# Both parts of the input in one product of 512 columns, joined at eviction

## The chip, the cores and the metric

The kernel runs on one core of a Trainium2 chip. The metric is the device time of one execution in microseconds (us), lower is better. The core's engines that matter here are TensorE (PE in the profile, with its weight loads shown apart as PEld), VectorE (DVE), ScalarE (ACT) and the DMA queue that SyncE (SP) issues to. Products are accumulated in PSUM, which has eight banks; a bank holds 512 fp32 values a partition. All other tiles are in SBUF.

## What is computed

Two layers of a hybrid network over 256 tokens (128 of context, 128 latent), `D_MODEL` = 2048, `DEPTH` = 2. Nearly all the arithmetic of a layer is a matrix product of an activation with a weight that is read from HBM once:

```python
h = rms_norm(x, p['g_mix']) * (1 + scale1) + shift1
z = h @ p['w_in']                                   # 2048 -> 10752
q, k, v, xr, xg, us, gl = jnp.split(z, offs, axis=-1)
...                                                 # attention, RG-LRU scan, S5 scan
ssm = ssm * jax.nn.sigmoid(ssm @ p['glu_w'] + p['glu_b'])
merged = (g[:, :, 0] * (attn @ p['w_pa']) + g[:, :, 1] * (rec @ p['w_pr'])
          + g[:, :, 2] * (ssm @ p['w_ps']))
x = x + gate1 * (merged @ p['w_o'])
a, b = jnp.split(h2 @ p['w_up'], 2, axis=-1)        # h2: second norm
x = x + gate2 * ((jax.nn.gelu(dwconv_centred(a, ...)) * b) @ p['w_down'])
```

Scale, shift and gate come from a modulation product with `w_mod` (2048 -> 12288 a layer). All is fp32.

## The kernel before

**Split products.** To get fp32 accuracy out of the one-pass format `float32r`, each operand is kept as two parts: a rounded one (hi) and the rest (lo). For each contraction tile of 128 the kernel makes three products into one PSUM tile of 128 outputs x 256 tokens: weight-hi x input-hi, weight-hi x input-lo, weight-lo x input-hi. In all three the weight part (128 x 128) is the stationary operand and the input part (128 x 256) streams. `mm3` writes this for a unit of 16 contraction tiles (48 products, one bank); `unit2` for two output tiles of 8 contraction tiles each (24 products in each of two banks):

```python
a, b = xh(kt), xl(kt)
self.mm(pt, hi[:, c], a, kt == 0, False)
self.mm(pt, hi[:, c], b, False, False)
self.mm(pt, lo[:, c], a, False, kt == KT - 1)
```

The input's hi and lo parts lie in different tiles: `H0`/`H1` (hi) and `H2`/`H3` (lo) for the normed input, `brh`/`brl` for a branch's result, `hh`/`hl` for the hidden layer, `xas` for the input that is used before its norm is known (`early`).

**The stream of weights.** `run_items` walks a list of items. A "w" item is a unit; a "mod" item is one piece of the modulation product (into PSUM tile `ps_md`, four products of 32 rows side by side in plain fp32, which the trace records as eight); `filler` puts about 0.9 of them after each unit. Each half of a unit's weights (512 KB) is loaded by SP into one of six `raw` buffers (`emit_dma`), split by ACT (`whi`, a CAST, L115) and DVE (`wlo`, a subtraction, L71) in `emit_split`; three pairs of split buffers exist, so the split of a half waits until PE has read the half three before.

**Evictions.** The result of a unit is taken out of PSUM one item later (`later(1, ...)`), by a function that belongs to the unit: a tanh or a copy on ACT, a multiply-add on DVE, several instructions in some. Tag `mm` has two banks, so a bank has to be free two banks later. Evictions read PSUM (`ps_mm`) directly.

**Side work.** Between units `feed` advances generators that issue the S5 scan (`s5_gen`, in layer 0 also its tables, `s5_prep`), the attention and the RG-LRU scan, mostly DVE and some ACT work, at fixed steps a unit. The order on each engine is then made by a scheduler.

The stages by time in the trace: start-up to 160 us; layer 0's input projection, branches and S5 to 760; the rest of layer 0's mixing part and its channel part (`w_up`, `w_down`) to 1640; layer 1's mixing part to 2330; its rest to 3124.

Of the kernel before, what the change touches and what calls it, by code (L numbers as in the profile page):

```python
# [5 lines left out]
F32 = mybir.dt.float32  # L6
F32R = mybir.dt.float32r
# [4 lines left out]
P = 128  # L12
L = 2
D = 2048
KT = 16
# [18 lines left out]
class Builder:  # L34
# [150 lines left out]
    def emit_split(self, i, h):  # L185
        """parts of half a unit for the fp32r products; False while the buffers are still to be read"""
# [110 lines left out]
    # standard K=2048 unit, one 128-wide output tile  # L297
    def unit(self, src, xh, xl, evac):
# [6 lines left out]
    def mm3(self, pt, hv, xh, xl):  # L305
        for kt in range(KT):
            hi, lo = hv[kt // 8]
            c = slice((kt % 8) * P, (kt % 8 + 1) * P)
            a, b = xh(kt), xl(kt)
# [5 lines left out]
    def unit2(self, src, xh, xl, evac):  # L315
        def mm(hv):
            for t in range(2):
                pt = self.ps("mm", [T], 2)
                for kt in range(8):
                    hi, lo = hv[t]  # L320
                    c = slice(kt * P, (kt + 1) * P)
                    a, b = xh(kt), xl(kt)
                    self.mm(pt, hi[:, c], a, kt == 0, False)
                    self.mm(pt, hi[:, c], b, False, False)
                    self.mm(pt, lo[:, c], a, False, kt == 7)
                self.later(1, lambda t=t, pt=pt: evac(t, pt))
# [6 lines left out]
    def mod_mm(self, pt, raw, g, a, start, stop):  # L333
        """four contraction tiles at once, each in its own rows; only the first rows of a group are of use"""
# [17 lines left out]
    def mod_chunk(self, v, q, then):  # L352
        """two output tiles of a vector of layer 0, for use at once"""
# [22 lines left out]
    def startup(self, begin, evs, begin2, evs2):  # L376
        """the first norm, the S5 input and the first heads of layer 0, as the chunks of its scale and shift come in"""
# [21 lines left out]
        for q in range(8):  # L399
# [11 lines left out]
            def mm(hv, q=q):  # L411
                xh, xl = self.hx()
                for j in range(2):
                    hi, lo = hv[j]
                    kt = 2 * q + j
                    for f in range(8):
                        c = slice(f * P, (f + 1) * P)
                        self.mm(acc[f], hi[:, c], xh(kt), kt == 0 and f % 2 == 0, False, skip_group_check=True)
                        self.mm(acc[f], hi[:, c], xl(kt), False, False, skip_group_check=True)
                        self.mm(acc[f], lo[:, c], xh(kt), False, kt == KT - 1, skip_group_check=True)  # L420
# [9 lines left out]
            def mm2(hv, q=q):  # L430
                xh, xl = self.hx()
                for j in range(4):
                    hi, lo = hv[j // 2]
                    kt = 2 * q - 2 + j
                    for f in range(4):
                        c = slice((4 * (j % 2) + f) * P, (4 * (j % 2) + f + 1) * P)
                        self.mm(acc[8 + f], hi[:, c], xh(kt), kt == 0 and f % 2 == 0, False, skip_group_check=True)
                        self.mm(acc[8 + f], hi[:, c], xl(kt), False, False, skip_group_check=True)
                        self.mm(acc[8 + f], lo[:, c], xh(kt), False, kt == KT - 1, skip_group_check=True)
# [66 lines left out]
    def h_begin(self):  # L506
        self.H = [self.st(f"H{j}", [8, T], F32R, name=f"h{j}") for j in range(4)]
# [27 lines left out]
    def norm_part(self, l, which, kts, rs=None):  # L535
# [4 lines left out]
        for kt in kts:  # L540
            t = self.XA[kt // 8][:, kt % 8, :]
            hi, lo = self.H[kt // 8][:, kt % 8, :], self.H[2 + kt // 8][:, kt % 8, :]
# [1036 lines left out]
```

## Time and profile before

| | |
|---|---|
| time, median of 3 runs | 3125.14 us (3122.89 to 3130.1) |
| span of the profiled execution | 3124.1 us |
| PE busy / PEld busy | 98% / 91% of the span |
| DVE busy / ACT busy | 68% / 50% |
| mean granted TensorE clock | 0.997 of 2.4 GHz |
| HBM traffic | 231 GB/s over the span |

The span runs from the first to the last instruction of the profiled execution; what lies around it is about 1 us of the median. A busy share counts overlapping instructions once. Matmuls overlap one another, so PE's busy share says that a product was always under way, not that the engine was at its peak: the rate is read from the distance between the starts of successive products. Windows are given in us from the start of the span.

### The profile page before, as it was taken

The numbers are of one execution on the slowest core, as the hardware profiler recorded it, in microseconds if no ns is written. First come the engines' busy times: TensorE is split into PE (matmuls) and PEld (weight loads), VectorE is DVE, ScalarE is ACT, GpSimd is POOL, SyncE is SP. The second block draws the span as 40 slices with busy tenths as digits, with TensorE's granted clock in tenths as the row PEclk, the third lists the DMA queues.
The fourth block names the chain that finished last, engine by engine and source line by source line (L and its number), as shares of the span: only waits on it lengthen the run. The fifth ranks groups of instructions, "written<-read, shape, count | busy, mean of one in ns | idle before, by whom it ended". The sixth has DMA issues, their size and how long they took to land.

```text
span 3124.1 us, 66739 instructions
## 1 busy us (share of the span) xinstructions
PE 3063.2 (98%) x27745; PEld 2831.5 (91%) x27745; DVE 2125.4 (68%) x3864; ACT 1558.4 (50%) x2434; POOL 45.9 (1%) x87
## 2 busy tenths in 40 slices
PE   5899999999999999999999999999999999999999
PEld 4788888998999999999998888888999999999999
DVE  6478899989465766667557677877644766555554
ACT  4455767345445643344456446674334565434443
POOL 0000000000000000000000000000000000000000
PEclk9999999999999999999999999999999999999999
DMA  9865666667777777777777777777775546555553
GB/s 351 322 205 191 209 210 216 214 223 247 254 236 234 269 264 257 257 264 250 271 258 246 244 248 235 255 252 267 266 256 197 184 164 212 179 188 177 185 186 129
DMA packets 188542, 724.48 MB, mean 232 GB/s; under 512 B 21520, under 2 KB 22064, under 8 KB 179280
## 3 DMA queue, kind: packets, MB, share of 16 engines
q1 hardware_dynamic: 180576, 691.95, 65.0%
q0 software_dynamic: 7664, 28.27, 2.4%
q8 instruction: 218, 3.57, 0.4%
q14 instruction: 84, 0.69, 0.1%
HBM read 704.46 MB, written 15.68 MB: 231 GB/s over the span
## 4 chain that ended last, share of the span: by engine, by line
PE 87%; DVE 3%; ACT 2%; DMA 2%; issue 1%; SPq 0%; DVEq 0%; ACTq 0%
PE ps_mm L118 77%; PE ps_md L118 5%; PE ps_aux L118 2%; DMA raw<-in_w_in 2%; PE ps_y L118 1%; PE ps_v L118 1%; DVE wlo L71 1%; ACT whi L115 1%; PE ps_v L121 0%; ACT ltmp L111 0%; DVE t L71 0%; ACT xa L111 0%; PE ps_aux L121 0%; DVE xs L925 0%; DVE blk L71 0%
## 5 line engine op out<-in xcount | busy, mean ns | idle before, releaser
L118 PE MATMUL ps_mm<-h,whi 128*128 128x256 f32 x9824 | 1807.3, 286 | 5.8 <-ACT whi L115 4.1
L118 PEld LDWEIGHTS ps_mm<-h,whi 128*128 128x128 f32 x9824 | 1531.0, 192 | 90.7 <-issue 59.6
L115 ACT CAST whi<-raw 128x1024 fp32r<-128x1024 f32 x896 | 936.8, 1046 | 1303.1 <-PE ps_mm L118 1100.1
L71 DVE TENSOR_TENSOR wlo<-raw,whi 128x1024 fp32r<-128x1024 f32 x896 | 1095.3, 1223 | 684.8 <-ACT whi L115 662.6
L118 PE MATMUL ps_mm<-h,wlo 128*128 128x256 f32 x4912 | 1392.5, 284 | 9.3 <-DVE wlo L71 9.3
L118 PEld LDWEIGHTS ps_mm<-h,wlo 128*128 128x128 f32 x4912 | 942.4, 192 | 14.7 <-DVE wlo L71 11.7
L118 PE MATMUL ps_mm<-hh,whi 128*128 128x256 f32 x1024 | 292.8, 286 | 0.0
L118 PE MATMUL ps_mm<-hl,whi 128*128 128x256 f32 x1024 | 289.7, 283 | 0.0
L118 PE MATMUL ps_mm<-hh,wlo 128*128 128x256 f32 x1024 | 289.6, 283 | 0.0
L118 PE MATMUL ps_mm<-brh,whi 128*128 128x256 f32 x896 | 257.8, 288 | 0.0
L118 PE MATMUL ps_mm<-brl,whi 128*128 128x256 f32 x896 | 254.3, 284 | 0.0
L118 PE MATMUL ps_mm<-brh,wlo 128*128 128x256 f32 x896 | 253.1, 283 | 0.0
L118 PEld LDWEIGHTS ps_mm<-hh,whi 128*128 128x128 f32 x1024 | 196.2, 192 | 11.9 <-issue 11.1
L118 PE MATMUL ps_md<-raw,SC 128*32 128x256 f32 x2560 | 201.5, 389 | 2.1 <-issue 1.9
L118 PEld LDWEIGHTS ps_mm<-hl,whi 128*128 128x128 f32 x1024 | 196.4, 192 | 0.0
L118 PEld LDWEIGHTS ps_mm<-hh,wlo 128*128 128x128 f32 x1024 | 196.4, 192 | 0.0
L118 PEld LDWEIGHTS ps_mm<-brh,whi 128*128 128x128 f32 x896 | 171.4, 191 | 17.4 <-issue 10.7
L118 PEld LDWEIGHTS ps_mm<-brl,whi 128*128 128x128 f32 x896 | 171.6, 192 | 0.9 <-issue 0.8
L118 PEld LDWEIGHTS ps_mm<-brh,wlo 128*128 128x128 f32 x896 | 171.5, 192 | 0.1
L84 DVE SCALAR_TENSOR_TENSOR x<-ps_mm,MOD,x 128x128 f32<-128x128 f32 x192 | 58.6, 347 | 69.0 <-PE ps_mm L118 69.0
L118 PEld LDWEIGHTS ps_md<-raw,SC 128*32 128x32 f32 x2560 | 58.3, 108 | 46.2 <-issue 14.0
L111 ACT ACT_TABLE_LOAD x73 | 93.7, 1283 | 11.2 <-DVE sm L84 4.1
(238 smaller groups left out, 2631.6 us busy)
## 6 DMA issues: line engine op xcount, KB each, us to landing
raw<-in_w_mod SPq DMA_DIRECT2D x384, 512.0 KB, 5.1
raw<-in_w_in SPq DMA_DIRECT2D x304, 512.0 KB, 5.1
raw<-in_w_up SPq DMA_DIRECT2D x166, 512.0 KB, 4.5
raw<-in_w_up SPq DMA_DIRECT2D x45, 1024.0 KB, 4.9
raw<-in_w_down SPq DMA_DIRECT2D x90, 512.0 KB, 4.6
raw<-in_w_o SPq DMA_DIRECT2D x64, 512.0 KB, 4.6
raw<-in_w_down SPq DMA_DIRECT2D x19, 1024.0 KB, 4.9
raw<-in_w_pa SPq DMA_DIRECT2D x32, 512.0 KB, 5.1
```

What stands on the lines that cost most here:

```text
L71: self.nc.vector.tensor_tensor(out=out, in0=a, in1=b, op=op)
L84: self.nc.vector.scalar_tensor_tensor(out=out, in0=a, scalar=s, in1=b, op0=op0, op1=op1)
L111: self.nc.scalar.activation(out, a, func, **k)
L115: self.nc.scalar.copy(out, a)
L118: self.nc.tensor.matmul(out, lhsT, rhs, start=start, stop=stop, **k)
```

## The change

`unit`, `unit2` and `early` no longer issue two products with the weight's hi part. The input's two parts lie side by side (`split`: tiles of 4 contraction tiles x 2 parts x 256), and one product of 512 columns makes both, into the two halves of a bank that is now used whole. The product with the weight's lo part is added onto the first half (`mmx`); in the last contraction tile it goes first. At eviction `joined` copies the second half to SBUF by ACT and adds the first half to it by DVE; the unit's own eviction then reads that SBUF tile (`pj`) in place of PSUM. The start-up's products (`mmy`) and those of the V projection stay three of 256 columns.

```diff
     def unit(self, src, x, evac):
         def mm(hv):
-            pt = self.ps("mm", [T], 2)
-            self.mm3(pt, hv, xh, xl)
-            self.later(1, lambda: evac(pt))
+            pt = self.ps("mm", [2, T], 2)
+            self.mm3(pt, hv, x)
+            self.later(1, lambda: evac(self.joined(pt)))
...
-            self.mm(pt, hi[:, c], a, kt == 0, False)
-            self.mm(pt, hi[:, c], b, False, False)
-            self.mm(pt, lo[:, c], a, False, kt == KT - 1)
+            self.mmx(pt, hi[:, c], lo[:, c], x(kt), kt == 0, kt == KT - 1)
+    def mmx(self, pt, hi, lo, x, first, last):
+        if last:
+            self.mm(pt[:, 0, :], lo, x[:, 0, :], False, False)
+        self.mm(pt, hi, x, first, last)
+        if not last:
+            self.mm(pt[:, 0, :], lo, x[:, 0, :], False, False)
...
+    def joined(self, pt):
+        t = self.k1("pj")
+        self.acp(t, pt[:, 1, :])
+        self.add(t, pt[:, 0, :], t)
+        return t
+
+    def split(self, tags, name):
+        ts = [self.st(t, [4, 2, T], F32R, name=name) for t in tags]
+        return lambda kt: ts[kt // 4][:, kt % 4]
...
     def unit2(self, src, x, evac):
-                pt = self.ps("mm", [T], 2)
+                pt = self.ps("mm", [2, T], 2)
...
-                self.later(1, lambda t=t, pt=pt: evac(t, pt))
+                self.later(1, lambda t=t, pt=pt: evac(t, self.joined(pt)))
...
     def h_begin(self):
-        self.H = [self.st(f"H{j}", [8, T], F32R, name=f"h{j}") for j in range(4)]
+        self.H = self.split([f"H{j}" for j in range(4)], "h")
...
             def out():
                 t = box["t"] = self.k1("ee")
-                self.acp(t, pt)
+                self.acp(t, pt[:, 1, :])
+                self.add(t, pt[:, 0, :], t)
```

Over the whole program there are 6,912 products of 512 columns in place of twice as many of 256, and 482 joins (one ACT copy and one DVE addition each).

PE in the last part of layer 1, where one unit of `w_down` ends and the next begins (`ps_mm` is the bank, `hh`/`hl` are hidden-hi and hidden-lo, the column at the end is the product's size). Before:

```order
L118 MATMUL ps_mm_37130<-hh1_34204,whi_37119 128x256
L118 MATMUL ps_mm_37130<-hl1_34206,whi_37119 128x256
L118 MATMUL ps_mm_37130<-hh1_34204,wlo_37120 128x256
L118 MATMUL ps_mm_37186<-hh0_34203,whi_37123 128x256
L118 MATMUL ps_mm_37186<-hl0_34205,whi_37123 128x256
L118 MATMUL ps_mm_37186<-hh0_34203,wlo_37124 128x256
```

The same place in the changed kernel (`hid` holds both parts):

```order
L118 MATMUL ps_mm_31690<-hid_29364,wlo_31677 128x256
L118 MATMUL ps_mm_31690<-hid_29364,whi_31676 128x512
L118 MATMUL ps_mm_31690<-hid_29364,wlo_31677 128x256 x2
L118 MATMUL ps_mm_31690<-hid_29364,whi_31676 128x512
L118 MATMUL ps_mm_31733<-hid_29361,whi_31680 128x512
L118 MATMUL ps_mm_31733<-hid_29361,wlo_31681 128x256
```

Three products and three loads of weights a contraction tile became two and two, and the unit ends with a product of 512.

DVE in layer 0's first branch, at the eviction of the seventh `unit2` of `w_pa` (`mg` is the merged sum, `tg` the gate, `H`, `t`, `blk`, `FIN` belong to the S5 scan and its tables). Before:

```order
L71 TENSOR_TENSOR H<-pc,pd 128x2x130 x2
L84 SCALAR_TENSOR_TENSOR mg_3292<-tg,ps_mm 128x256
L71 TENSOR_TENSOR wlo<-raw,whi 128x1024
L95 COPY FIN<-H 128x4
L71 TENSOR_TENSOR t_5415<-blk,TINY 128x512
L71 TENSOR_TENSOR t_5416<-blk,TINY 128x512
L84 SCALAR_TENSOR_TENSOR mg_3292<-tg,ps_mm 128x256
L71 TENSOR_TENSOR blk<-t_5415,t_5416 128x256 x2
```

In the changed kernel:

```order
L71 TENSOR_TENSOR wlo<-raw,whi 128x1024
L95 COPY FIN<-H 128x4
L71 TENSOR_TENSOR t_4975<-blk,TINY 128x512
L71 TENSOR_TENSOR t_4976<-blk,TINY 128x512
L71 TENSOR_TENSOR pj<-ps_mm,pj 128x256
L71 TENSOR_TENSOR blk<-t_4975,t_4976 128x256 x2
L84 SCALAR_TENSOR_TENSOR mg_3110<-tg,pj 128x256
L71 TENSOR_TENSOR pj<-ps_mm,pj 128x256
L71 TENSOR_TENSOR wlo<-raw,whi 128x1024
L84 SCALAR_TENSOR_TENSOR mg_3110<-tg,pj 128x256
```

Each of the two evictions has got an addition of its own ahead of the multiply-add, and the bank is released by that addition.

## Rows read from the trace of the kernel before

**Rows 1.** Page, part 1: busy time of each engine, share, instructions.

```profile
PE 3063.2 (98%) x27745; PEld 2831.5 (91%) x27745; DVE 2125.4 (68%) x3864; ACT 1558.4 (50%) x2434; POOL 45.9 (1%) x87
```

**Rows 2.** Chain that ended last, 2330 to 3124 us: start, duration, engine, count.

```profile
2330.32 230.39 PE ps_mm L118 x1920
```

**Rows 3.** Busy time by stage; after the engines clock, DMA share, GB/s.

```profile
0.00:160.00 160.00, 120.31 (x1108) 94.65 (x1109) 83.49 (x257) 68.39 (x145) 4.30 (x11) 0.95 0.89 336
160.00:330.00 170.00, 167.51 (x1515) 147.87 (x1513) 137.30 (x285) 93.56 (x167) 3.40 (x6) 1.00 0.58 191
330.00:760.00 430.00, 426.33 (x4191) 385.30 (x4189) 397.03 (x853) 252.47 (x377) 11.29 (x21) 1.00 0.66 221
760.00:1640.00 880.00, 880.00 (x7848) 811.92 (x7847) 554.34 (x988) 399.76 (x618) 16.80 (x31) 1.00 0.75 256
1640.00:2330.00 690.00, 680.11 (x6460) 604.60 (x6460) 492.79 (x848) 371.99 (x597) 8.45 (x15) 1.00 0.75 253
2330.00:3124.00 794.00, 788.94 (x6636) 787.16 (x6634) 460.49 (x636) 372.25 (x534) 1.61 (x3) 1.00 0.54 180
```

**Rows 4.** The same stretches, instructions on tile ps_mm alone: PE, PEld, DVE, ACT.

```profile
160.00:330.00 170.00, 125.39 (x960) 117.67 (x960) 12.22 (x26) 10.17 (x24) 1.00 0.58 191
330.00:760.00 430.00, 344.74 (x2743) 332.38 (x2744) 12.33 (x30) 16.29 (x43) 1.00 0.66 221
760.00:1640.00 880.00, 805.85 (x6439) 779.40 (x6438) 77.00 (x201) 25.91 (x52) 1.00 0.75 256
1640.00:2330.00 690.00, 541.84 (x4262) 518.87 (x4261) 25.32 (x58) 31.53 (x81) 1.00 0.75 253
2330.00:3124.00 794.00, 785.91 (x6529) 784.08 (x6528) 77.88 (x203) 26.61 (x54) 1.00 0.54 180
```

**Rows 5.** Timeline of PEld near 284 us, loads for plain fp32 products of 512 columns.

```profile
283.65 0.19 PEld L118 LDWEIGHTS ps_aux<-attf,kv 128*128 128x128 f32 x1 [0.24 <-issue]
284.08 0.19 PEld L118 LDWEIGHTS ps_aux<-attf,kv 128*128 128x128 f32 x1 [0.24 <-issue]
```

**Rows 6.** Timeline of PE: four plain fp32 products of 256, then twelve of 1.

```profile
412.63 1.02 PE L118 MATMUL ps_aux<-xc,gw 128*128 128x256 f32 x4
...
171.56 1.48 PE L118 MATMUL ps_aux<-CST,sqq 128*128 128x1 f32 x12
```

**Rows 7.** Groups of PE by form: last, mean ns of one product.

```profile
L118 PE MATMUL ps_mm<-hl,whi 128*128 128x256 f32 x1024 | 289.7, 283 | 0.0
L118 PE MATMUL ps_aux<-xc,gw 128*128 128x256 f32 x128 | 32.9, 384 | 2.5 <-ACT ltmp L111 2.5
L121 PE MATMUL ps_v<-CST,S 128*128 128x128 f32 x128 | 19.4, 273 | 2.0 <-ACT vs L115 1.5 <-DVE pb L71 0.5
L118 PE MATMUL ps_aux<-CST,sqq 128*128 128x1 f32 x64 | 8.7, 247 | 2.5 <-ACT sqq L111 2.3
```

**Rows 8.** Groups by form of ACT and DVE that stand for the join.

```profile
L115 ACT COPY kv<-ps_mm 128x256 f32<-128x256 f32 x8 | 2.7, 368 | 0.0
L71 DVE TENSOR_TENSOR fa<-fa,ps_mm 128x256 f32<-128x256 f32 x62 | 26.1, 420 | 35.2 <-PE ps_mm L118 35.2
L71 DVE TENSOR_TENSOR hl<-fa,hh 128x256 fp32r<-128x256 f32 x64 | 26.7, 419 | 1.0 <-ACT hh L115 1.0
```

**Rows 9.** Busy time in the two stretches where DVE is fullest.

```profile
510.00:560.00 50.00, 49.66 (x461) 44.94 (x454) 49.62 (x105) 30.73 (x48) 0.55 (x1) 1.00 0.66 223
710.00:760.00 50.00, 49.18 (x488) 43.69 (x487) 49.01 (x129) 26.97 (x43) 1.61 (x3) 1.00 0.73 248
```

**Rows 10.** Chain that ended last, 1640 to 1800 us, around one wait.

```profile
1729.87 0.61 PE ps_md L118 x8
1730.49 0.02 issue
1730.50 6.55 DMA raw<-in_w_in
```

**Rows 11.** Timeline of ACT and DVE, 2700 to 2709 us: splits and evictions in w_up.

```profile
2700.10 1.05 ACT L115 CAST whi<-raw 128x1024 fp32r<-128x1024 f32 x1 [1.88 <-PE ps_mm L118]
2701.17 1.23 DVE L71 TENSOR_TENSOR wlo<-raw,whi 128x1024 fp32r<-128x1024 f32 x1 [1.70 <-ACT whi L115]
2702.93 1.05 ACT L115 CAST whi<-raw 128x1024 fp32r<-128x1024 f32 x1 [1.32 <-PE ps_mm L118]
```

More of the change, by code (lines that the diff above doesn't have):

```diff
@@ L295, in run_items, with unit, mm3 @@
         self.run_pending(10 ** 9)
-    def unit(self, src, xh, xl, evac):
+    def unit(self, src, x, evac):
         def mm(hv):
-            pt = self.ps("mm", [T], 2)
-            self.mm3(pt, hv, xh, xl)
-            self.later(1, lambda: evac(pt))
+            pt = self.ps("mm", [2, T], 2)
+            self.mm3(pt, hv, x)
+            self.later(1, lambda: evac(self.joined(pt)))
         self.items.append(dict(ffn=self.ffn, kind="w", src=src, mm=mm))
-    def mm3(self, pt, hv, xh, xl):
+    def mm3(self, pt, hv, x):
         for kt in range(KT):
@@ L308, in mm3, with mmy, unit2 @@
             c = slice((kt % 8) * P, (kt % 8 + 1) * P)
-            a, b = xh(kt), xl(kt)
-            self.mm(pt, hi[:, c], a, kt == 0, False)
-            self.mm(pt, hi[:, c], b, False, False)
-            self.mm(pt, lo[:, c], a, False, kt == KT - 1)
-    def unit2(self, src, xh, xl, evac):
+            self.mmx(pt, hi[:, c], lo[:, c], x(kt), kt == 0, kt == KT - 1)
[5 more added lines that the diff above has]
+            self.mm(pt[:, 0, :], lo, x[:, 0, :], False, False)
+    def mmy(self, pt, hi, lo, x, first, last, **k):
+        self.mm(pt, hi, x[:, 0, :], first, False, **k)
+        self.mm(pt, hi, x[:, 1, :], False, False, **k)
+        self.mm(pt, lo, x[:, 0, :], False, last, **k)
+    def joined(self, pt):
[6 more added lines that the diff above has]
+        return lambda kt: ts[kt // 4][:, kt % 4]
+    def unit2(self, src, x, evac):
         def mm(hv):
             for t in range(2):
-                pt = self.ps("mm", [T], 2)
+                pt = self.ps("mm", [2, T], 2)
                 for kt in range(8):
@@ L417, in mm @@
                         c = slice(f * P, (f + 1) * P)
[L418 to L420 removed]
+                        self.mmy(acc[f], hi[:, c], lo[:, c], x(kt), kt == 0 and f % 2 == 0, kt == KT - 1, skip_group_check=True)
                 def out():
@@ L565, in xa_begin @@
             return
-        xs = [self.st(t, [8, T], F32R, name="xas") for t in split]
-        self.XSPL = (lambda kt: xs[kt // 8][:, kt % 8, :]), (lambda kt: xs[2 + kt // 8][:, kt % 8, :])
+        self.XSPL = self.split(split, "xas")
     def xa(self, kt):
@@ L574, in xa @@
         if self.XSPL:
[L575 removed]
+            h = self.XSPL(kt)
+            self.hilo(h[:, 0], h[:, 1], t)
     def early(self, l, which, src, evac):
@@ L611, in early, with br_begin, bx @@
         return scale, lambda: evac(box["t"])
+    def br_begin(self):
+        self.BR = [self.st(t, [4, 2, T], F32R, name="br") for t in ("B0", "B1")]
+    def bx(self, kt):
+        return self.BR[kt // 4][:, kt % 4]
     def hx(self):
-        return (lambda kt: self.H[kt // 8][:, kt % 8, :]), (lambda kt: self.H[2 + kt // 8][:, kt % 8, :])
+        return lambda kt: self.H(kt)
     def setup(self):
@@ L1314, in ev @@
                 self.xa(o)
-            self.unit(d["w_o"][l, o], hx[0], hx[1], ev)
+            self.unit(d["w_o"][l, o], hx, ev)
             self.filler(1)
@@ L1327, in hid_begin @@
             def hid_begin():
-                self.HID = [self.st("A0", [8, T], F32R, name="hh0"), self.st("A1", [8, T], F32R, name="hh1"),
-                            self.st("B0", [8, T], F32R, name="hl0"), self.st("B1", [8, T], F32R, name="hl1")]
+                self.HID = self.split(("A0", "A1", "B0", "B1"), "hid")
             evs = []
@@ L1360, in layer @@
                     self.seg = 3
-                self.unit(evs[k][0], hx[0], hx[1], evs[k][1])
+                self.unit(evs[k][0], hx, evs[k][1])
                 self.filler(1)
@@ L1382, in ev @@
                             q.dma_start(dst[:, o + 1 - w:o + 1, :], self.X[o // 8][:, (o + 1 - w) % 8:(o + 1 - w) % 8 + w, :])
-                self.unit(d["w_down"][l, hf, o], dx[0], dx[1], ev)
+                self.unit(d["w_down"][l, hf, o], lambda kt: self.HID(kt), ev)
                 self.filler(1)
@@ L1405, in win_unit @@
     def win_unit(self, l, c, hx, ev):
-        self.unit(self.d["w_in"][l, c], hx[0], hx[1], ev)
+        self.unit(self.d["w_in"][l, c], hx, ev)
         self.filler(1)
```

67 lines of the change are left out of this document (30 added, 37 removed).

## The prediction

> **What bounds the kernel now.** I read the page's busy shares first, then the chain of waits, then a table by stage. PE is busy 98% of the span, DVE 68%, ACT 50% [rows 1]. In the last part of layer 1 the chain is PE alone, 1,920 products in 230.39 us, so 0.120 us from one start to the next [rows 2]. The stages differ [rows 3]. From 760 to 1640 and from 2330 to 3124 PE is the bound: DVE holds 554 of 880 us and 460 of 794. From 330 to 760 PE and DVE are both full: DVE holds 397 of 430 us, and 49.6 and 49.0 of 50 in its fullest stretches [rows 9]. From 1640 to 2330 DVE holds 493 of 690 us, and the chain goes now and then through a weight load that lands late, 6.55 us after its issue [rows 10]. The start-up keeps its products, so nothing is taken from it.
>
> The split products make up most of PE's work. By the rows on their PSUM tile [rows 4] there are 960 from 160 to 330, 2,743 from 330 to 760, 6,439 from 760 to 1640, 4,262 from 1640 to 2330 and 6,529 after. With the V projection's 96 a layer taken out and divided by three, these are 288, 914, 2,146, 1,389 and 2,176 contraction tiles, 6,913 together; the changed program has 6,912 products of 512. Each contraction tile costs 3 x 0.120 = 0.360 us now.
>
> **What a product of 512 columns costs.** No such product of this format is in the trace. Three neighbours bound it. Plain fp32 products of 512 columns start 0.43 us apart (284.08 less 283.65), and their weight loads leave PEld idle 0.24 us each [rows 5]; four of 256 columns take 1.02 us with about 0.38 for the last, so 0.213 apart [rows 6, 7]. So plain fp32 time is proportional to columns, 0.83 ns each, with 2 or 3 ns left over. Twelve products of one column take 1.48 us with 0.247 for the last [rows 6, 7], 0.112 apart: that is what a load of 128 x 128 takes when nothing else is to be done. One split product at half the plain time per column would be 0.107 us, and measures 0.120. The 13 ns above can be
>
> - the load (0.112) that hardly fits beside 0.107 us of columns. Then 512 columns hide it, and the pair of products costs half of 0.43 and 0.120, so 0.335 us: 25 ns saved a contraction tile;
> - a fixed cost a product. Then the pair costs 0.227 and 0.120, so 0.347: 13 ns saved;
> - a slower rate per column in this format. Then 512 columns cost 0.240, and nothing is saved but perhaps the 3 ns that plain products leave over.
>
> The durations of single products speak for something of the product's own: 283 ns for a split product against 273 for a plain one of 128 columns, whose columns also take 0.107 us [rows 7], so some 10 ns, with the load the same size. That is against the first reading in part, and leaves the second and third. The first two agree that 512 columns are better than twice 256, by 13 to 25 ns; I take 18, nearer to the row on durations, so 0.342 us a pair.
>
> **The rest of the change.** Each of the 482 results costs ACT a copy of half a bank, 0.368 us, and DVE an addition of 0.420 [rows 8]: 177 us of ACT and 202 of DVE over the kernel. What the unit's own eviction reads from SBUF in place of PSUM I cost at nothing, since a subtraction on SBUF tiles of 256 columns runs 0.419 us, as long as the product with PSUM beside it [rows 8].
>
> - **760 to 1640 and 2330 to 3124** (PE-bound, 4,322 contraction tiles): 4,322 x 18 ns = 78 us less. The join lies beside PE's work: a half's weights are split by a CAST of 1.05 us and a subtraction of 1.23 us, which end 2.3 us after the third half before is read [rows 11], and they are needed two halves (5.76 us) after it. The copy and the addition stand ahead of them in ACT's and DVE's queue and take at most 0.9 us of those 3.4. A bank is needed again one unit later, and is free a little over 1 us after the last product. If that cover were gone, each join would cost PE its 0.8 us, 386 us over the 482.
> - **160 to 330**: 288 x 18 ns = 5 us; DVE rises from 137 to about 145 of 170, I take 4 less.
> - **330 to 760**: PE could save 914 x 18 ns = 16 us. But DVE gets 73 joins (30 evictions on DVE and 43 on ACT read the tile there, one instruction each [rows 4]) x 0.420 = 31 us, and its 397 us become 428 in a stretch of 430. Queued behind each addition are the weight's lo part and the S5 scan, and PE waits for the lo part. In its fullest stretches DVE reached 0.98 to 0.99 of the time, over the whole stage 0.92. At 0.99 the stage lasts 432 us, at 0.92 it lasts 465; I take 0.96, so 446: 16 us more.
> - **1640 to 2330**: 1,389 x 18 ns = 25 us, DVE has room. Where the chain goes through a late load, a faster PE only waits longer, so I keep half: 12 us less. The order in which SP issues loads stays as it is, and each load is freed by the same split.
> - **Ends**: the last result needs the copy and the addition ahead of the two multiply-adds, 0.8 us, and at the three places where a norm waits for the last result of a sum the same is paid once: 4 us together.
>
> The sum is 3124 - 78 - 4 + 16 - 12 + 4 = 3050 us of span; the median of the runs lies 1 us above the profiled span, so 3051.
>
> **Rivals.**
>
> 1. *The load is the whole excess* (0.335 a pair). Then the parts are 108, 6 and 17 us less, the stage from 330 to 760 costs 14 more (DVE bound either way), the ends 4: 3011 us of span, 3012. For it: a lone load takes 0.112 us, and in each plain product of 512 it is hidden by far. Against: the 10 ns in the durations. The Trainium skill, "TensorE: Matmul & The Clock Gate", section "Back-to-back issue gap", gives N/2.4 + 2.5 ns for an isolated product on a warm clock, 216 ns at 512 columns. By the page a pair would be 0.336 and the sum the same as here; the plain rows agree with its 2.5 ns (0.43 for twice 512 columns' time), the split product of 256 does not (0.120 against 109 ns by the page).
> 2. *DVE binds wherever the scan runs.* The stage from 330 to 760 goes on at DVE's 0.92, so 35 us more, and layer 1's mixing part gains nothing: 3124 - 78 - 2 + 35 + 4 = 3083, 3084 us. For it: DVE's queue is in order and an addition now waits for ACT's copy, so waits are added with the work. Against: the scheduler sets the additions between other work.
> 3. *The format's rate per column is the limit* (a pair stays at 0.357 to 0.360). Then PE-bound stages give 0 to 13 us, and the joins cost DVE's full stage 17 to 20 us, layer 1's mixing part up to 5, and 4 at the ends: 3132 to 3153 us, about 3142, so slower than before. It decides from a pair of about 0.355 us: 4,322 x 5 ns no longer pays the 22 us. For it: the trace has one size of split product only, and 0.120 / 256 would do as a rate. Against: nothing else suggests so odd a rate, 1.12 times half of the plain one.
> 4. *The wide product is not one product on the chip.* The trace has each plain fp32 product twice as often as the program: 128 on the RG-LRU gates [rows 7], where the program issues 64. If a wide split product ran as two of 256 with a load each, nothing would be saved and the joins paid: 3153 us. Against: split products of 256 stand in the trace once each, the 6,913 contraction tiles of [rows 4] show it.
>
> **Chances.** The forecast 0.38 (3035 to 3080), the load 0.22, DVE 0.12, the rate 0.25, two products 0.03. The likeliest gives 3051 us. The range goes from 3005, below the load's 3012, to 3150, which takes in most of the rate's cases; some 0.12 is left out. A measurement of this kernel can tell about 0.2% (6 us) from no change. Faster by more than that: the first three and little of the rate, 0.73. Within it: the better end of the rate, 0.08. Slower: 0.19.
>
> **What would show it.** In the changed profile the chain from 2330 on should be PE again, with starts 0.215 to 0.230 us apart after a product of 512 and about 0.120 after one of 256: that pair decides between the readings, and 0.24 would make the prediction wrong. PE's loads should be a third fewer on the split products. DVE's busy time should be about 2,330 us and ACT's 1,735. The stage that ends at 760 should end at 765 to 800; if it ends before 755, DVE was not full. From 330 to 760 waits of PE for the weights' lo part should appear; in the PE-bound stages there should be none.

## The result and the profile after

The changed kernel takes 3088.51 us (median of four runs, 3087.64 to 3091.02), the kernel before, timed beside it, 3124.01 us (3119.44 to 3130.1). The ratio is 0.9881, with a 95% interval of 0.9865 to 0.9896: 1.2% faster. The forecast was 3051 us, the range 3005 to 3150. So the sign and the range held, and about half of the forecast gain came: the profiled span went from 3124.1 to 3085.9 us, 38 us less where the sum had 74.

The busy shares, page part 1 of after (for [rows 1]):

```profile
span 3085.9 us, 53872 instructions
PE 3022.0 (98%) x20833; PEld 2443.8 (79%) x20833; DVE 2280.2 (74%) x4352; ACT 1700.4 (55%) x2910; POOL 45.8 (1%) x87
```

6,912 products and as many weight loads are gone (27,745 to 20,833), and PE is still busy 98% of the span: it had 25% fewer instructions and lost 1.3% of its busy time. DVE rose by 155 us and ACT by 142 us.

Busy time by stage in after, the stretches cut where the work of [rows 3] ends (columns: stretch, length, PE, PEld, DVE, ACT, POOL, granted clock, DMA share, GB/s):

```profile
0.00:157.00 157.00, 117.80 (x1105) 92.59 (x1106) 83.55 (x257) 68.08 (x144) 4.30 (x11) 0.96 0.89 342
157.00:327.00 170.00, 167.86 (x1240) 133.65 (x1239) 143.82 (x310) 99.09 (x185) 3.39 (x6) 0.99 0.58 194
327.00:757.00 430.00, 423.44 (x3271) 333.95 (x3270) 411.50 (x911) 274.30 (x450) 11.29 (x21) 1.00 0.65 220
757.00:1623.00 866.00, 863.04 (x5677) 687.79 (x5677) 601.76 (x1139) 441.50 (x755) 16.79 (x31) 1.00 0.75 259
1623.00:2297.00 674.00, 669.49 (x5079) 524.56 (x5078) 527.07 (x952) 404.12 (x699) 8.46 (x15) 1.00 0.76 259
2297.00:3086.00 789.00, 780.40 (x4470) 671.26 (x4468) 512.54 (x786) 413.30 (x681) 1.61 (x3) 1.00 0.53 182
```

The lengths of before were 160, 170, 430, 880, 690 and 794 us. The first surprise is the third row: the stage that was to be held up by DVE is as long as before, with DVE at 411.5 of 430. The second is the last row: 2,176 contraction tiles with PE as the bound gave 5 us by these cuts (8 by the marks of the table below), where 39 were forecast.

The chain of waits from 2700 to 3000 us in after is one piece (start, duration, engine, count):

```profile
2699.99 300.09 PE ps_mm L118 x1699
```

So PE alone, as in [rows 2], but 300.09 / 1,699 is 0.1766 us a product, 0.3533 us a pair of a wide and a narrow one. Before it was 0.360. The timeline of PE shows how the pair divides (start, duration):

```profile
2900.57 0.40 PE L118 MATMUL ps_mm<-h,whi 128*128 128x512 f32 x1
2900.81 0.28 PE L118 MATMUL ps_mm<-h,wlo 128*128 128x256 f32 x1
2900.93 0.40 PE L118 MATMUL ps_mm<-h,whi 128*128 128x512 f32 x1
2901.17 0.28 PE L118 MATMUL ps_mm<-h,wlo 128*128 128x256 f32 x1
2901.29 0.40 PE L118 MATMUL ps_mm<-h,whi 128*128 128x512 f32 x1
```

0.24 us from the start of a wide product to the next, 0.12 after a narrow one. Over all pairs on this tile the starts mostly lie 230 to 241 ns apart after a wide product (median 236) and 113 to 120 after a narrow one (median 117). A pair saves 360 - 353.3 = 6.7 ns, not 18; over 6,912 of them that is 46 us. So the products gave 46 us and, net, something took 8 back. Part of it shows in the waits of PE and PEld (waiting tile and line, released by; us in total, times, longest):

```profile
PE ps_mm L118 <- DVE pj L71: 5.9, 10, 1.2
PEld ps_mm L118 <- ACT pj L115: 36.4, 87, 1.0
PEld ps_mm L118 <- DVE pj L71: 21.6, 45, 1.7
```

`pj` is the tile of the join, and nothing like it stood in before. PEld's waits may be covered by the product that runs meanwhile, those of PE are not. By windows, PE's 5.9 us are 2.4 from 330 to 760 us, 0.9 from 1640 to 2300, 1.6 from 2300 to 2442 and one wait of 1.0 at the norm that follows; from 760 to 1640 there is none. But for the last, these are stretches with units of 1024 rows (`unit2`: `w_glu` and the three branch projections `w_pa`, `w_pr` and `w_ps`), where a bank takes 8 contraction tiles only. From 760 to 1640 such units stand too (layer 0's `w_glu` and `w_ps`), but with pieces of the modulation product between them, which give a bank more time. In layer 1's `w_glu` and `w_ps`, from 2300 to 2442, there are no such pieces; the same part of before had no wait of PE at all. Three timelines around 2412 us, in `w_ps` of layer 1, show one (start, duration, instruction, idle time before it). ACT:

```profile
2412.67 1.05 ACT L115 CAST whi<-raw 128x1024 fp32r<-128x1024 f32 x1 [1.50 <-issue]
2413.62 0.36 ACT L115 COPY pj<-ps_mm 128x256 f32<-128x256 f32 x1
```

DVE at the same place:

```profile
2413.75 1.22 DVE L71 TENSOR_TENSOR wlo<-raw,whi 128x1024 fp32r<-128x1024 f32 x1 [0.31 <-ACT whi L115]
2414.89 0.42 DVE L84 SCALAR_TENSOR_TENSOR h<-mg,h 128x256 fp32r<-128x256 f32 x1
2415.23 0.42 DVE L71 TENSOR_TENSOR pj<-ps_mm,pj 128x256 f32<-128x256 f32 x1
```

PE, the rows at the change from bank to bank:

```profile
2412.20 0.88 PE L118 MATMUL ps_mm<-br,whi 128*128 128x512 f32 x2
2415.26 1.00 PE L118 MATMUL ps_mm<-br,whi 128*128 128x512 f32 x2
```

The two rows of PE are the last wide product of one bank and the first of the next; two of them in a row take 0.63 us where nothing is waited for (0.236 from start to start and 0.40 for the second), so 0.25 and 0.37 us are wait. Such waits are mostly too short for the list above, since the product before them still counts as running: at the 37 changes of bank from 2300 to 2450 us that have two wide products in a row, the starts lie 4.9 us further apart, added up, than at 0.236 each; in e2, e4 and e7 below the same sum is nothing. A bank's last product starts at 2412.20. ACT's copy starts at 2413.62, behind the CAST of the next weights in ACT's queue, DVE's addition at 2415.23, behind that weight's low part, and the bank is free at 2415.65, 3.2 us after the last product has had its 0.24. It is needed 8 pairs after that, 2.8 us. In the units of 2048 rows the same join has 16 pairs, 5.65 us.

### The profile page after: what moved, and what is told of

It is laid out like the page before. It is cut to its first block, busy times and chain, and to the rows that moved or that the text cites. A ratio compares the mean times of both kernels' runs of the same rounds, so it can differ in the third digit from the quotient of the medians.

```text
span 3085.9 us, 53872 instructions
## 1 busy us (share of the span) xinstructions
PE 3022.0 (98%) x20833; PEld 2443.8 (79%) x20833; DVE 2280.2 (74%) x4352; ACT 1700.4 (55%) x2910; POOL 45.8 (1%) x87
## 5 line engine op out<-in xcount | busy, mean ns | idle before, releaser
L118 PE MATMUL ps_mm<-h,whi 128*128 128x512 f32 (+1 forms) x4976 | 1772.3, 400 | 10.0 <-DVE pj L71 4.7
L118 PEld LDWEIGHTS ps_mm<-h,whi 128*128 128x128 f32 x4976 | 925.9, 189 | 286.5 <-issue 29.1
L115 ACT COPY pj<-ps_mm 128x256 f32<-128x256 f32 x479 | 175.6, 367 | 377.5 <-PE ps_mm L118 377.3
L118 PE MATMUL ps_mm<-hid,whi 128*128 128x512 f32 x1024 | 364.5, 401 | 0.0
L118 PE MATMUL ps_mm<-br,whi 128*128 128x512 f32 x896 | 324.8, 405 | 2.1 <-DVE pj L71 1.2
L71 DVE TENSOR_TENSOR pj<-ps_mm,pj 128x256 f32<-128x256 f32 x479 | 200.8, 420 | 124.7 <-ACT pj L115 124.2
L118 PE MATMUL ps_mm<-hid,wlo 128*128 128x256 f32 x1024 | 277.0, 281 | 0.0
L118 PE MATMUL ps_mm<-br,wlo 128*128 128x256 f32 x896 | 233.9, 282 | 0.0
L118 PEld LDWEIGHTS ps_mm<-hid,whi 128*128 128x128 f32 x1024 | 190.3, 188 | 53.5 <-ACT pj L115 7.8
L118 PEld LDWEIGHTS ps_mm<-hid,wlo 128*128 128x128 f32 x1024 | 193.3, 189 | 4.7
```

What stands on the lines that cost most here:

```text
L71: self.nc.vector.tensor_tensor(out=out, in0=a, in1=b, op=op)
L115: self.nc.scalar.copy(out, a)
L118: self.nc.tensor.matmul(out, lhsT, rhs, start=start, stop=stop, **k)
```

## The experiments

All times below are medians; before was timed in the same rounds (3126.2, 3128.4 and 3125.4 us in the three groups of runs). The table gives, from each trace, the time between the starts of the products with the weight's low part in the 289th, 1,203rd, 3,349th, 4,738th and 6,912th contraction tile (about the stages of [rows 3], free of the start-up; the V projection's 64 tiles are counted, so there are 6,976, and in before the marks stand at 293, 731, 1614, 2305 and 3097 us), and, apart, of tiles 5,001 to 5,201, which are layer 1's `w_ps`, 16 results of 8 tiles, with some four units of 2048 rows around it. Each row is one execution; e1's is the slowest of its six and e2's of its four (6 and 5 us above their medians). The rows of e10 and e11, which are after and e3 once more, show how far such a row repeats: within 1.7 us.

| kernel | 289 to 1,203 | to 3,349 | to 4,738 | to 6,912 | 5,001 to 5,201 |
|---|---|---|---|---|---|
| before | 438.4 | 883.0 | 690.8 | 792.5 | 72.0 |
| after | 437.4 | 873.9 | 674.1 | 784.2 | 75.5 |
| e10, after again | 437.7 | 872.6 | 675.5 | 784.0 | 75.5 |
| e1, join alone | 439.8 | 892.5 | 696.7 | 798.1 | 75.5 |
| e2, products alone | 433.6 | 868.9 | 679.3 | 781.6 | 70.6 |
| e3, long units only | 436.0 | 870.7 | 676.2 | 778.7 | 71.5 |
| e11, e3 again | 435.6 | 870.0 | 677.9 | 778.5 | 71.5 |
| e4, bank copied | 439.2 | 878.3 | 675.8 | 776.7 | 70.6 |
| e7, one instruction | 437.3 | 869.5 | 680.1 | 777.0 | 70.7 |
| e8, e3 and e7 | 437.9 | 870.1 | 682.7 | 778.0 | 71.5 |
| e5, bfloat16 | 430.7 | 815.1 | 648.7 | 725.8 | 70.6 |
| e6, bfloat16, three products | 428.2 | 810.3 | 668.2 | 723.0 | 65.5 |
| e9, bfloat16, long units only | 421.3 | 814.3 | 648.5 | 718.4 | 65.3 |

### The two parts of the change apart

**e1**: the join without the wide product.

```diff
-        if last:
-            self.mm(pt[:, 0, :], lo, x[:, 0, :], False, False)
-        self.mm(pt, hi, x, first, last)
-        if not last:
-            self.mm(pt[:, 0, :], lo, x[:, 0, :], False, False)
+        self.mm(pt[:, 0, :], hi, x[:, 0, :], first, False, skip_group_check=True)
+        self.mm(pt[:, 1, :], hi, x[:, 1, :], False, last, skip_group_check=True)
+        self.mm(pt[:, 0, :], lo, x[:, 0, :], False, last, skip_group_check=True)
```

> The changed kernel with its joins, but with three products of 256 columns a contraction tile as before; the input's low part goes into the second half of the bank. Theory A (the trace of after: starts 236 ns apart after a product of 512 and 117 after one of 256, so a pair saves 360 - 353 = 6.7 ns; 6,912 of them are 46 us, of which the joins eat about 8): all starts 120 ns apart again, 3124 + 8, so 3128 to 3140 us. Rival B (the joins cost far more, and the pairs saved more than the starts say, as forecast): 3150 us or more. Rival C (the joins lie wholly beside PE's work): 3124, within 6 us of before.

Measured: 3144.73 us, ratio 1.0052 (1.0038 to 1.0066), so 18 us slower than before. The chain from 2700 to 3000 us is again one of PE alone at 0.120 us a product:

```profile
2699.98 300.11 PE ps_mm L118 x2499
```

The joins cost more than theory A had, and are not free. The column for tiles 5,001 to 5,201 shows a part of it: 3.5 us in these 20 joins. Another part is not the join's own work: from 1174 to 1179 us, after a pause of PE, the granted clock is 0.66, taken up below.

**e2**: the wide product without the join; evictions read the first half.

```diff
-        t = self.k1("pj")
-        self.acp(t, pt[:, 1, :])
-        self.add(t, pt[:, 0, :], t)
-        return t
+        return pt[:, 0, :]
...
-                self.acp(t, pt[:, 1, :])
-                self.add(t, pt[:, 0, :], t)
+                self.acp(t, pt[:, 0, :])
```

> The changed kernel's products, but no join: evictions read the first half of the bank, as before. The share of the input's low part times the weight's high part is left out of the results. Theory A: 3124 - 46 = 3078 us of span (3070 to 3086); the difference from after is what the joins cost, about 8. Rival B (joins and the waits for a bank eat most of the gain): 3040 to 3060. Rival C (joins cost nothing): 3086 to 3089, the same as after.

Measured: 3079.56 us, ratio 0.9851 (0.9837 to 0.9865), 46.6 us under before. Theory A had 46 from the starts alone. The wide product is worth what its starts say, all of it on the path to within the 4 us that the ratio leaves open, in the stage with a full DVE too (4.8 of 438 us, for 914 x 6.7 ns = 6.1). That settles the main question: no gain of 124 us (6,912 x 18 ns) was made and eaten; it was never there. After is 9 us slower than e2, e1 18 us slower than before; the two parts add up to 28 us less than before, and the whole has 33 to 36 (two timings). Each ratio is known to 4 or 5 us, so the joins' cost is 9 to 18 us and no better known from these.

### What the join costs, and where

**e3**: the units of 1024 rows go back to three products without a join.

```diff
 def unit2
-                pt = self.ps("mm", [2, T], 2)
+                pt = self.ps("mm", [T], 2)
-                    self.mmx(pt, hi[:, c], lo[:, c], x(kt), kt == 0, kt == 7)
-                self.later(1, lambda t=t, pt=pt: evac(t, self.joined(pt)))
+                    self.mmy(pt, hi[:, c], lo[:, c], x(kt), kt == 0, kt == 7)
+                self.later(1, lambda t=t, pt=pt: evac(t, pt))
```

> The changed kernel, but the units of 1024 rows (two outputs a unit: w_glu, w_ps and the two projections of the RG-LRU) go back to three products of 256 with no join. In after PE waits there for a bank, up to 0.5 us a join in ACT's and DVE's queue. 896 pairs give back 896 x 6.7 ns = 6 us; 128 joins go. Theory A (the waits for the bank cost 8 us or more in these units): 3078 to 3087 us, no slower than after. Rival C (these waits only take the place of others): 3092 to 3095 us, 6 above after.

Measured: 3081.16 us, ratio 0.9855 (0.9842 to 0.9868). The units that go back are `w_glu`, `w_pa`, `w_pr` and `w_ps`, with 112 joins (896 / 8); the expectation counts 128, and has the RG-LRU's two projections for `w_pa` and `w_pr`. Because this and the changed kernel had been timed in different groups, both were run again side by side, as e10 (the changed kernel, no edit) and e11 (e3, no edit):

> The changed kernel itself, once more, on the same chip and in the same rounds as e11, since e3's 3,081 us and the changed kernel's 3,088 us were taken apart. 3,087 to 3,091 us.

> The kernel of e3 once more. Theory A (in the units of 1024 rows the wait for the bank costs more than the wide product saves, 6 us): 6 to 8 us below e10. Rival C (e3's 7 us were the difference of two chips): within 3 us of e10.

Measured: 3092.01 us, ratio 0.9894 (0.988 to 0.9909), and 3080.93 us, ratio 0.986 (0.9845 to 0.9875). The changed kernel is 1 us above what was expected, and the difference 11 us where 6 to 8 were. So giving up 13% of the wide products (896 of 6,912) makes the kernel 7 us (first timing) to 11 us (side by side) faster; some 3 us of the 11 lie ahead of the 289th tile, which the edit doesn't touch. The waits of PE on the join in e3, for the line of after above (5.9 us in 10 waits):

```profile
PE ps_mm L118 <- DVE pj L71: 1.2, 2, 1.0
```

**e4**: the bank is copied whole by ACT, and DVE adds from SBUF.

```diff
-        t = self.k1("pj")
-        self.acp(t, pt[:, 1, :])
-        self.add(t, pt[:, 0, :], t)
+        b = self.st("pb", [2, T], name="pbank", bufs=1)
+        self.acp(b, pt)
+        self.add(b[:, 0, :], b[:, 0, :], b[:, 1, :])
+        return b[:, 0, :]
...
-        return self.st("k1", [T], name=name, bufs=6)
+        return self.st("k1", [T], name=name, bufs=5)
```

To make room, one of the six `k1` buffers is given up, and a small tile of the early norm shares the one staging tile.

> The changed kernel, but ACT copies the whole bank (512 columns) to SBUF and DVE adds the halves there, so that a bank is free after one instruction and PE never waits for DVE. Theory A (PE waits for the bank because the addition stands behind other work in DVE's queue): the waits of PE on pj from DVE go, 3080 to 3086 us. Rival C (the wait is for ACT as much as for DVE; a copy of 512 columns takes 0.2 us longer, and one staging tile instead of several holds the next join back): 3089 to 3100 us.

Measured: 3090.83 us, ratio 0.9886 (0.9873 to 0.9898): no better than after. Yet the waits did go: tiles 5,001 to 5,201 take 70.6 us, as with no join at all, and layer 1's last stage is 7.5 us shorter than in after. It was lost ahead of the 289th tile (3.2 us) and in layer 0, where the first two columns are 1.8 and 4.4 us longer. Whether the single staging tile, the buffer given up or the longer copy lost it, this run can't tell apart. One place can be read. The timeline of PE in e4:

```profile
518.24 0.50 PE L118 MATMUL ps_mm<-h,whi 128*128 128x512 f32 x1
521.23 0.58 PE L118 MATMUL ps_mm<-h,wlo 128*128 128x256 f32 x1 [2.48 <-DVE wlo L71]
```

The busy time of e4 around it (columns as in the table by stage, the clock third from the end):

```profile
518.00:521.00 3.00, 0.74 (x5) 0.22 (x4) 3.00 (x9) 1.65 (x4) 0.55 (x1) 0.77 0.57 175
521.00:526.00 5.00, 4.78 (x15) 4.10 (x16) 4.20 (x9) 2.44 (x5) 0.00 (x0) 0.50 0.57 188
```

PE stood still for 2.48 us, waiting for a weight's low part that DVE, busy all the time with the RG-LRU's scan, had in its queue; the granted clock fell within the pause and was 0.50, the lower of its two levels (1.2 of 2.4 GHz), for the next 5 us. So a pause can cost more than its own length. In after the same is seen at the norm before layer 0's channel sub-layer, in its busy time:

```profile
1158.00:1160.00 2.00, 0.00 (x0) 0.00 (x0) 1.97 (x8) 0.21 (x1) 0.00 (x0) 1.00 0.91 287
1160.00:1164.00 4.00, 3.89 (x19) 3.03 (x20) 2.66 (x7) 1.50 (x3) 0.55 (x1) 0.61 0.74 225
```

After an idle time of 2.35 us five pairs started 0.64 us apart in place of 0.353, so 1.4 us more. The timeline of PE there:

```profile
1160.91 0.63 PE L118 MATMUL ps_mm<-h,whi 128*128 128x512 f32 x1
1161.33 0.41 PE L118 MATMUL ps_mm<-h,wlo 128*128 128x256 f32 x1
1161.55 0.63 PE L118 MATMUL ps_mm<-h,whi 128*128 128x512 f32 x1
```

In e3 PE pauses 1.60 us at this place and the clock stays at 1.00; in e10, the same program as after, it pauses 2.24 us and the clock stays as well. The length of the one pause does not decide it. In before, layer 1's mixing part has a pause of 1.21 us that ends at 1762.91 and one of 2.28 that ends at 2074.59, and the clock falls after the shorter:

```profile
1763.00:1767.00 4.00, 4.00 (x24) 3.17 (x25) 3.90 (x6) 0.22 (x1) 0.00 (x0) 0.57 0.86 291
2075.00:2079.00 4.00, 4.00 (x43) 3.07 (x42) 2.17 (x7) 4.00 (x8) 0.00 (x0) 1.00 0.00 0
```

What decides it stays open here. Each fall is worth 1 to 3 us.

With these two things, PE's idle time (by the waits in the profile) and its time at the lower clock (of which half is lost), the columns of after can be added up against before:

| | 289 to 1,203 | to 3,349 | to 4,738 | to 6,912 |
|---|---|---|---|---|
| the pairs, at 6.7 ns | -6.1 | -14.4 | -9.3 | -14.6 |
| PE's idle time, before and after | 3.7, 6.0 | 0.0, 4.0 | 9.5, 3.8 | 1.7, 3.0 |
| at the lower clock, before and after | 0, 0 | 0, 3.4 | 3.4, 0 | 0, 0 |
| sum | -3.8 | -8.7 | -16.7 | -13.3 |
| measured | -1.0 | -9.1 | -16.7 | -8.3 |

The last column lacks 5.0 us, of which 3.3 are the short waits at the changes of bank in `w_ps` (the 4.9 above less 1.6 that count as idle); where the rest and the 2.8 us of the first column went was not traced. So the change lost 5 to 6 us of its pairs in each of three stretches, and got 7 us in layer 1's mixing part, where pauses that before had are shorter.

**e7**: the join as one instruction of DVE on the bank; **e8**: the same in e3.

```diff
-        self.acp(t, pt[:, 1, :])
-        self.add(t, pt[:, 0, :], t)
+        self.nc.vector.tensor_reduce(t, pt.rearrange("p a t -> p t a"), mybir.AxisListType.X, ALU.add)
```

> The changed kernel with the join as one DVE instruction, a sum over the two halves straight from the bank (512 elements read, 256 written), instead of ACT's copy and DVE's addition; ACT's 479 copies go. Theory A (PE waits for the bank because a join needs two queues, ACT's and then DVE's): waits of PE on the join shrink, 3,080 to 3,087 us. Rival B (DVE's time counts: the sum takes about 0.65 us in place of 0.42, 479 x 0.23 = 110 us more of DVE): the stage from 327 to 757, where DVE holds 411 of 430 us, grows by 10 or more and the time is 3,095 us or above.

Measured: 3086.52 us, ratio 0.9864 (0.9848 to 0.9881), which is not told apart from after. Page part 1 of e7:

```profile
PE 3021.7 (98%) x20833; PEld 2445.6 (79%) x20833; DVE 2400.2 (78%) x4352; ACT 1575.8 (51%) x2430; POOL 46.0 (1%) x87
```

The join itself, from the groups on tile `pj` (min, median and max ns, first and last start):

```profile
L328 DVE TENSOR_REDUCE pj<-ps_mm x479: 660/691/693, 171.9 to 3075.4; 128x256 f32<-128x512 f32 x160
```

DVE has 120 us more to do than in after, and the stage that was held to be DVE's lasts 437.3 us against 437.4. DVE's busy time there, in e7 (columns as above):

```profile
327.00:757.00 430.00, 427.28 (x3274) 334.74 (x3273) 421.98 (x885) 247.46 (x369) 10.79 (x20) 1.00 0.67 221
```

So in this format DVE can hold 422 of 430 us and the stage is no longer for it. Two effects lie in this run, more work of DVE and no wait of PE on a join (2.4 us in after); e8 below, against e3, has the first almost alone. Tiles 5,001 to 5,201 take 70.7 us: with one queue to pass instead of two, the bank is free in time.

> The kernel of e3 (units of 1024 rows back at three products of 256 without a join) with e7's join of one instruction in the rest. e3 took 3,081 us. Theory A: no bank is waited for in the units of 2048 rows (a bank is free again long before its next unit), so the form of the join does not matter there: 3,078 to 3,084 us. Rival B (DVE's time counts): 3,088 us or more.

Measured: 3087.24 us, ratio 0.9863 (0.9846 to 0.988): between the two expectations, 6 us above e3. By stage it loses to e3 1.9 us in the first and 6.5 in layer 1's mixing stage, nothing in the PE-bound ones. So DVE's extra work costs some 2 us in the stage that was held to be DVE's, hardly more than such a row repeats. In layer 1's mixing stage e7 loses 6.0 us to after in the same way. Most of both is pauses and the clock: PE's idle time there is 7.2 us in e8 and 4.8 in e3, 7.5 in e7 and 3.8 in after, and e8 and e7 have 6.8 us each at the lower clock, the others none. That the longer instruction makes these pauses is likely, but not shown: e2, with no join at all, has 8.8 and 6.8 us there.

### What sets the price of a product

**e5**: the parts in bfloat16. **e6**: the kernel before with the same edit.

```diff
-F32R = mybir.dt.float32r
+F32R = mybir.dt.bfloat16
-        self.sub(lo, src, hi.bitcast(F32))
+        self.sub(lo, src, hi)
...
```

Four more subtractions lose their `bitcast` in the same way.

> The changed kernel with the split parts in bfloat16 instead of the rounded fp32 format: same products (512 and 256 columns), same joins, same instructions; the parts hold fewer bits, so the results are less exact. Theory A (0.46 ns a column, seen in before as 120 ns at 256 and in after as 236 at 512, belongs to the 4-byte format): starts 214 and 108 ns apart, half of the plain fp32 product's 429 and 215; a pair saves some 30 ns, 6,912 of them 207 us at most, and DVE, which holds 411 of 430 us from 327 to 757, gives some of it back: 2,890 to 2,990 us. Rival C (the rate belongs to products with a new weight each time, whatever the format): starts stay at 236 and 117, 3,080 to 3,090 us.

> The kernel before (three products of 256, no join) with the parts in bfloat16. Under theory A three starts of 108 ns, or of 112 if the weight load (112 ns between one-column products in before) limits a product of 256 columns: 324 or 336 ns a contraction tile instead of 360. With 108 the wide product saves nothing in this format and this run is no slower than e5, 2,880 to 2,970 us; with 112 it is 30 to 80 us slower than e5. Rival C: 3,115 to 3,130 us.

Measured: 2928.78 us, ratio 0.9365 (0.935 to 0.938), and 2936.70 us, ratio 0.9389 (0.9372 to 0.9406). A piece of e5's chain of waits (start, duration, engine, count):

```profile
2593.18 249.76 PE ps_mm L118 x1536
```

And of e6's:

```profile
2448.41 476.68 PE ps_mm L118 x4365
```

e5: 0.1626 us a product, 0.3252 a pair; its starts are 216 ns apart after 512 columns and 109 after 256. e6: 0.1092 us a product, 0.3276 for three. So the 120 ns of before, and the 236 of after, belong to the 4-byte format; with 2-byte parts the same columns take half of the plain fp32 product's 0.43 and 0.213 us [rows 5, 6]. And the wide product saves 2.4 ns a pair there, against 6.7: the format that is slower a column is also the one with more to save. In time it saves nothing that can be seen: e5 is 8 us under e6, between the two cases of the expectation, but three of its four columns are longer, and it leads in layer 1's mixing part alone (19.5 us), where e6's PE idles 30 us and has 20 us at the lower clock, e5's 22 and 3. In e6 a product of 256 columns with a weight load of its own starts 109 ns after the last, so nothing of a load's 112 ns [rows 6] shows even there; the loads are shorter too (98 ns by their own rows, 192 in before), so this alone doesn't speak for the 4-byte ones, but their 236 ns at 512 columns, where a load is well hidden, do.

The Trainium skill, "TensorE: Matmul & The Clock Gate", section "Back-to-back issue gap", gives N/2.4 + 2.5 ns for an isolated product: 216 at 512 columns and 109 at 256. The bfloat16 parts agree to the nanosecond, the 4-byte parts (236 and 117 to 120) do not. The same section's 131 ns for a stream of products of 512 columns is seen in neither.

In the first stage e5 and e6 gained only 8 and 10 us, though PE's products there became 9% shorter: this is the stage where, with a faster PE, something else is late next. PE idles 24 us of it in each. DVE holds 0.96 of it in e5, by the busy time from 330 to 700 us:

```profile
330.00:700.00 370.00, 347.80 (x2868) 202.44 (x2866) 356.48 (x771) 240.94 (x393) 9.34 (x18) 1.00 0.68 220
```

**e9**: e5 with e3's edit.

> e5 (parts in bfloat16) with the units of 1024 rows at three products of 256 and no join, as in e3. In this format the wide product saves 2 ns a pair (216 + 109 against 3 x 109), 896 x 2 = 2 us given back; e5's waits of PE for a join's bank were 26 us in 35 waits of up to 2.6. If these waits cost what they show: 2,900 to 2,915 us; if most of them only take the place of other waits: 2,920 to 2,930.

Measured: 2907.64 us, ratio 0.9304 (0.9288 to 0.9319): 21 us under e5, as expected if the waits cost what they show. In e5 the waits of PE on the join had been (as above):

```profile
PE ps_mm L118 <- DVE pj L71: 26.4, 35, 2.6
```

The gain lies in the first and the last column (9.4 and 7.4 us); in layer 1's mixing part, where 8.9 us of these waits had been, there is none, and e9 has 10 us at the lower clock there, e5 3. The faster PE runs into the bank sooner, so the join costs more than in the 4-byte format. e9 is the fastest kernel of the study, at the price of parts with fewer bits; with the 4-byte parts and whole results it is e3.

## Why the prediction was right or wrong

**The bound** was read rightly: from 2300 to 2920 us the chain is PE's products for 91 to 98% in every kernel, and e2 shows that what is taken from a pair comes off the end, to within 4 us.

**The price of a pair** is the term that failed. It was put at 0.342 us and is 0.3533: the saving was 6.7 ns and not 18. Of the three readings of the 13 ns, the load (0.335) and the fixed cost (0.347) were both too low, and the third, a slower rate in this format (0.357 to 0.360), was off by 4 ns only. The two numbers 120 at 256 columns and 353.3 at 256 and 512 together are met by 6.7 ns a product and 0.443 ns a column; two numbers for two unknowns, so nothing tests this split. The working took half of the plain fp32 rate, 0.418 ns, as given, since "nothing else suggests so odd a rate". e5 and e6 show that this rate exists, but for 2-byte parts. The row that spoke for something of the product's own (283 ns against 273) was misread. The same products in 4-byte and in 2-byte parts, in after and in e5, by their groups (last, mean ns of one):

```profile
L118 PE MATMUL ps_mm<-hid,whi 128*128 128x512 f32 x1024 | 364.5, 401 | 0.0
L118 PE MATMUL ps_mm<-hid,whi 128*128 128x512 bf16 x1024 | 335.0, 379 | 0.9 <-DVE hid L71 0.8
L118 PE MATMUL ps_mm<-hid,wlo 128*128 128x256 f32 x1024 | 277.0, 281 | 0.0
L118 PE MATMUL ps_mm<-hid,wlo 128*128 128x256 bf16 x1024 | 268.8, 273 | 0.5 <-ACT hid L115 0.5
```

The 4-byte product lasts 8 ns longer at 256 columns and 22 at 512: the excess grows with the columns, as a rate does, and was no sign of a fixed cost. With 6.7 ns the PE-bound term is 4,322 x 6.7 = 29 us in place of 78.

**The join in the PE-bound stages** was called hidden, by the half-bank rhythm of `w_up`, where it is. In `unit2` a bank has 2.8 us, and the join's way through two queues takes 3.2. The working's own test, "a bank is needed again one unit later", was made for the units of 2048 rows and not for those of 1024. e1 and after show the loss at tiles 5,001 to 5,201 (3.5 us more than before, 5 more than without a join), e3, e4 and e7 that it goes in three different ways. A third bank for the tag `mm` might be a fourth way, which no run tried; by the kernel's tags the other six banks are in use. With the join's cost the PE-bound stages gave 9.1 + 8.3 = 17.4 us, where 78 were forecast.

**The stage from 330 to 760** was put at 16 us more, and gained 1. The 73 joins do take 30.5 us of DVE by their own row, but DVE's busy time rose by 14.5 (397.0 to 411.5): 15 other instructions moved out of the stretch, successive instructions overlap (in the timeline above, `h` at 2414.89 lasts 0.42 us and the next starts at 2415.23), and 33 idle us were there to take the rest. Over the kernel a join adds 155 / 488 = 0.32 us of DVE, and not 0.42 (479 joins on `pj` and 9 on `ee` stand in the trace, 488, where 482 were counted). More to the point, e7 put another 0.25 us of DVE on each join and the stage didn't move, and e8 lost 1.9 us there to e3. DVE's fullness was taken for a bound from two stretches of 50 us; it was no bound at this speed of PE. Rival 2, with 35 us there, falls with it.

**Layer 1's mixing part** gave 16.7 us for 12 forecast, though its 1,389 tiles are worth 9.3 by the measured price. e2 has 11.5 there and e3 14.6. The other 7.4 are pauses: PE idles 9.5 us there in before and 3.8 in after, and before has 3.4 us at the lower clock, which cost it half of that. Why after's pauses are shorter, no run shows, so this term came out near by luck.

**The start of the join at the ends** was put at 4 us; the last result costs 1.2 us more than before (4.7 us from the end of the last product to the end, 3.5 before). At the norm before layer 0's channel part PE idles 2.35 us in after, 1.68 in e2 without a join, and not at all in before. From 160 to 330 the 4 us came in after (the 289th tile is 4.1 us earlier), but in e10 only 1.8 did, so this term is not known better than that.

**The sum** came out nearer than its terms: 61 us too much gain in the PE-bound stages, 17 too much loss in DVE's, 5 too little gain in layer 1's, and 3 in the ends. That the wrong terms offset one another in part is luck. **The rivals**: rival 3 had the pair nearly right and its sign wrong, because it took over the same price for DVE's stage; by its own break-even (a pair of 0.355) the measured 0.353 is faster. Rivals 1 and 4 are out: the pair is 0.353 and the loads fell by 6,912.

**The signs named beforehand**: PE alone in the chain, yes but for the units of 1024 rows, where it goes through the join and the splits. Starts of 0.215 to 0.230 us, no: 0.236, nearer to the 0.24 that was to show it wrong. Loads a third fewer on the split products, yes. DVE about 2,330 and ACT 1,735 us: 2,280 and 1,700. End of the stage at 765 to 800: 757. More waits for the low part from 330 to 760: 2.1 us in two waits, 0.3 before (over the kernel 9.9 and 9.3). No waits in the PE-bound stages: there are, on `pj`.

## What to carry to other kernels

Don't halve the rate of one format to get that of another: a trace with one size of product can't divide its time into columns and a fixed cost, and the one size that is there, taken as a plain rate, is the safe bound (here it gives 0.360 a pair, and 0.353 was measured). An extra step between a PSUM bank and its release should be checked against the shortest life of a bank in the kernel, with the queues that it passes in order, and left out where the life is shorter than the way; that part of the change made it slower. An engine that is full in a busy row is a bound only if more work on it makes the stage longer, which one run with the work added can tell.

## What the runs showed of the hardware

- Split products of 4-byte parts with a new weight each: 120 ns at 256 columns, 236 ns (median) at 512; the starts after wide products vary (230 to 241, and 113 to 120 after the narrow one between them), while of runs of 256 alone nine in ten are 120. Of 2-byte parts: 109 and 216, nearly throughout.
- At the lower clock a 4-byte pair takes 0.64 us (after, 1160.91 to 1164.11 us, five pairs), so 0.833 ns a column with nothing left over; at the upper one it takes 0.353 and not half of 0.64. The excess of the 4-byte format shows at the upper clock alone.
- A join of ACT's copy and DVE's addition holds a bank for 0.37 and 0.42 us of work, but 3.2 us of time, when each stands behind a split of the next weights.
- DVE sums the two halves of a bank in one instruction in 0.69 us (median), 512 elements in and 256 out.
- After a pause of PE of 2.48 us (e4) the granted clock was 0.50 for 5 us, after one of 2.35 (after) 0.61 over 4 us, after one of 1.21 (before) 0.57 over 4 us; after 1.60 (e3), 2.24 (e10) and 2.28 us (before) it stayed at 1.00. So the length of a pause alone does not tell whether the clock falls.
